# The dense tiles' hidden state kept in SBUF through the expert mixer, and the first block of U in other slots

## The chip, the cores and the metric

The kernel runs on one core of one Trainium2 chip, as one program, written in Python with a scheduler that orders the instructions of five engines and places their waits. The metric is the device time of the whole program in microseconds (us), the median of three runs. Engine names in the rows: PE is TensorE (PEld its weight loads), DVE is VectorE, ACT is ScalarE, POOL is GpSimd, SP is SyncE, which issues most DMAs; a q behind a name (SPq, ACTq) is the engine's issuing queue.

## The reference

One decoder layer over 512 tokens of width 1024, in float32:

```python
mod = silu(c) @ w_ada + b_ada                       # shift, scale, gate, twice
h   = rms_norm(x, norm1_g) * (1 + scale1) + shift1
proj = h @ w_in                                      # latent attention and forgetting attention
o   = concat(latent_attention(proj), forgetting_attention(proj))
x   = x + gate1 * (o @ w_o)
h2  = rms_norm(x, norm2_g) * (1 + scale2) + shift2
qp  = h2 @ w_pq                                      # 8 heads x 2 halves x 128
sc  = qp . sub_keys                                  # 128 keys per half
# top 16 of each half, top 16 of their sums -> 16 experts of 16384 per head and token
x   = x + gate2 * sum_e softmax(top)_e * gelu(peer_u[e] . h2) * peer_v[e]
```

## The kernel before, in words

The 512 tokens are four tiles of 128. Tile 0 is "sparse": its experts' rows of `peer_u` and `peer_v` are gathered from DRAM by GpSimd (L831) and used on VectorE (L849, L859). Tiles 1 to 3 are "dense": for all 384 tokens together TensorE computes every expert's `peer_u . h2` in 128 blocks of 128 experts (the U blocks, `dense_u`), and then the gated sum with `peer_v` in 128 blocks (`v_mm`, L981). A gate matrix G, built from the chosen experts, is written to DRAM and read back between the two.

Float32 products are three products of two rounded parts: ScalarE casts the high part (`hi`), VectorE subtracts it (`lo`), and TensorE runs hi·hi, hi·lo, lo·hi. For weights this is `halves` (L371 load, L373 `whi`, L374 `wlo`, products L385 to L387), for h2 L724 and L725, for a U or V block `split` (L871 `uhi`, L872 `ulo`), with the products of a U block in L935 to L937: 24 matmuls of 128x384.

The stages in order of time: a start (adaLN vectors, the first normalised tiles), projections and attention to 390 us, the queries (`queries`: four chunks of `w_pq`, 96 products of 128x384 each, then scores with the sub keys, L666), the U blocks (from 490 us to 1049 us), and the V blocks. The top 16 searches on VectorE (`top16`, L731 to L735) of the dense tiles run beside the queries and the first U blocks.

The order on each engine is made by the scheduler, which places an instruction when its operands and a slot for its result are there by its own clock; on the chip each engine then runs its list in that order and waits where a semaphore has not come. A DMA also waits until an older DMA that used the same of eight completion semaphores has landed. So a smaller pool or an absent DMA can move instructions far from the edited lines.

Memory around the change: `k4` is a pool of 28 slots of 4 KB per partition. It holds the split weights, and the mask, the rope table, the values `V` of the four tiles, and h2. `k4` is closed (`reopen`) when the U blocks begin, and the pool "dense" is opened in its place. h2 therefore goes to DRAM (`hd`) when it is made, 24 DMAs of 128 KB on ScalarE's queue (L727), and comes back into the new pool as `hhi` and `hlo`, 8 DMAs of 384 KB on GpSimd's queue (L884). The first U block is loaded in `reopen` too, after the pool has opened.

## Time and profile before

| | us |
|---|---|
| median of 3 runs (lowest, highest) | 1693.03 (1692.58, 1693.55) |
| the profiled execution | 1691.5 |
| its span in the trace | 1689.1 |
| TensorE busy | 1586.1 (94%) |
| VectorE busy | 1263.2 (75%) |
| ScalarE busy | 678.6 (40%) |
| GpSimd busy | 478.6 (28%) |

The time of an execution is about 2.4 us more than the span that the trace covers. Shares are averages over stages that have different limits: a stage is read from a window of its own, and from what ended the idle time in front of an engine's instructions.

### The profile page before, as it was taken

The page shows a single profiled execution, that of the slowest core. Times are in us where ns is not written, and L with a number is a line of the kernel's source. Part 1 is how long each engine was busy: PE and PEld are TensorE (multiplying, and loading weights), DVE is VectorE, ACT ScalarE, POOL GpSimd, SP SyncE. Part 2 cuts the span into 40 slices and gives each one's busy share as a digit, 9 for nine tenths or more (in the row PEclk, how much of TensorE's full clock was granted, in tenths as well). Part 3 has the DMA queues.
Part 4 walks back from the last instruction along what each step waited for, and adds up shares of the span by engine and source line. Part 5 has one row for each costly group of instructions (what it writes and reads, how often), then busy time and mean ns, then how long its engine had stood idle before and what let it go on. Part 6 is the DMA issues. An engine that isn't in the chain of part 4 may idle for free.

```text
span 1689.1 us, 25030 instructions
## 1 busy us (share of the span) xinstructions
PE 1586.1 (94%) x8993; PEld 1390.9 (82%) x8993; DVE 1263.2 (75%) x2626; ACT 678.6 (40%) x1072; POOL 478.6 (28%) x514
## 2 busy tenths in 40 slices
PE   5999999998978999999999999799999999999996
PEld 2976498987977999999999999787777777877885
DVE  2624364585899679899989899488888888887863
ACT  3522364354224434334656656333333333333331
POOL 1303510001013355564213232123333333233311
PEclk8999999999989999999999999999999999999998
DMA  7354513368154688888999999999999999999852
GB/s 295 122 212 159 194 39 132 121 215 272 36 188 139 229 287 264 262 281 270 346 335 337 328 325 349 387 354 368 353 370 357 366 365 358 366 375 364 289 180 100
DMA packets 189391, 451.34 MB, mean 267 GB/s; under 512 B 16594, under 2 KB 102610, under 8 KB 185172
## 3 DMA queue, kind: packets, MB, share of 16 engines
q1 hardware_dynamic: 91732, 277.17, 46.1%
q0 software_dynamic: 38656, 139.48, 23.5%
q10 hardware_dynamic: 58880, 33.11, 6.5%
q8 instruction: 70, 1.15, 0.3%
q14 instruction: 53, 0.43, 0.1%
HBM read 393.07 MB, written 56.63 MB: 266 GB/s over the span
## 4 chain that ended last, share of the span: by engine, by line
PE 75%; DVE 11%; DMA 7%; ACT 2%; issue 2%; POOL 0%; POOLq 0%; SPq 0%; DVEq 0%; ACTq 0%
PE acc L981 27%; PE bank L937 8%; PE bank L936 8%; PE bank L935 8%; PE bank L386 4%; PE bank L173 4%; PE bank L387 4%; PE bank L385 4%; DVE ulo L872 3%; PE bank L820 3%; DMA vt<-in_peer_v 2%; PE bank L136 2%; PE bank L564 2%; PE bank L579 2%; DMA ge<-ged 1%
## 5 line engine op out<-in xcount | busy, mean ns | idle before, releaser
L981 PE MATMUL acc<-vhi,whl 128*128 128x512 f32 x1536 | 422.6, 395 | 25.7 <-ACT vhi L871 17.0
L981 PEld LDWEIGHTS acc<-vhi,whl 128*128 128x128 f32 x1536 | 289.0, 189 | 94.1 <-ACT vhi L871 21.7
L937 PE MATMUL bank<-hhi,ulo 128*128 128x384 f32 x1024 | 348.0, 340 | 17.2 <-DVE ulo L872 17.2
L935 PE MATMUL bank<-hhi,uhi 128*128 128x384 f32 x1024 | 346.3, 339 | 12.3 <-ACT uhi L871 12.2
L936 PE MATMUL bank<-hlo,uhi 128*128 128x384 f32 x1024 | 348.3, 340 | 0.0
L831 POOL DMA_INDIRECT gat<-in_peer_v,ids x128 | 158.4, 1238 | 348.2 <-DVE y L859 324.2
L871 ACT CAST uhi<-ut 128x1024 fp32r<-128x1024 f32 x128 | 134.5, 1051 | 304.5 <-PE bank L936 262.4
L981 PE MATMUL acc<-vlo,whl 128*128 128x512 f32 x768 | 241.0, 395 | 0.1
L831 POOL DMA_INDIRECT gat<-in_peer_u,ids x128 | 142.6, 1114 | 336.0 <-DVE sact L849 305.1
L872 DVE TENSOR_TENSOR ulo<-ut,uhi 128x1024 fp32r<-128x1024 f32 x128 | 178.5, 1395 | 63.6 <-ACT uhi L871 62.8
L937 PEld LDWEIGHTS bank<-hhi,ulo 128*128 128x128 f32 x1024 | 194.3, 190 | 23.0 <-DVE ulo L872 22.6
L935 PEld LDWEIGHTS bank<-hhi,uhi 128*128 128x128 f32 x1024 | 194.3, 190 | 14.2 <-ACT uhi L871 13.8
L936 PEld LDWEIGHTS bank<-hlo,uhi 128*128 128x128 f32 x1024 | 194.5, 190 | 0.5
L872 DVE TENSOR_TENSOR vlo<-vt,vhi 128x1024 fp32r<-128x1024 f32 x128 | 156.4, 1222 | 43.6 <-ACT vhi L871 42.7
L871 ACT CAST vhi<-vt 128x1024 fp32r<-128x1024 f32 x128 | 133.7, 1049 | 110.6 <-PE acc L981 85.4
L981 PEld LDWEIGHTS acc<-vlo,whl 128*128 128x128 f32 x768 | 145.1, 189 | 33.1 <-DVE vlo L872 1.2
L859 DVE SCALAR_TENSOR_TENSOR y<-gat,swgt,y 128x1024 f32<-128x1024 f32 x127 | 167.8, 1322 | 1.8 <-DMA gat<-in_peer_v,ids 1.7
L971 ACT CAST whl<-ge 128x384 fp32r<-128x384 f32 x128 | 65.4, 512 | 257.4 <-PE acc L981 240.1
L849 DVE CUSTOM_DVE_ANT_0 scr<-gat,h2r 128x1024 bf16<-128x1024 f32 x128 | 166.2, 1298 | 0.1
L972 DVE TENSOR_TENSOR whl<-ge,whl 128x384 fp32r<-128x384 f32 x128 | 70.8, 555 | 55.6 <-ACT whl L971 52.4
L822 ACT ACTIVATE gst<-bank 128x512 f32<-128x512 f32 x96 | 96.8, 1117 | 9.3 <-PE bank L820 4.7
L968 DVE TENSOR_TENSOR ge<-ge,gt 128x384 f32<-128x384 f32 x128 | 69.8, 552 | 17.7 <-DMA ge<-ged 15.6
(252 smaller groups left out, 2217.2 us busy)
## 6 DMA issues: line engine op xcount, KB each, us to landing
ut<-in_peer_uT SPq DMA_DIRECT2D x128, 512.0 KB
vt<-in_peer_v SPq DMA_DIRECT2D x128, 512.0 KB
G<-gst ACTq DMA_DIRECT2D x24, 1024.0 KB
gt<-G SPq DMA_DIRECT2D x16, 1536.0 KB
ged<-ge SPq DMA_DIRECT2D x120, 192.0 KB
ge<-ged SPq DMA_DIRECT2D x120, 192.0 KB
w<-in_w_ada SPq DMA_DIRECT2D x16, 1024.0 KB
w<-in_w_pq SPq DMA_DIRECT2D x32, 512.0 KB
```

The costliest lines, as they stand in the source:

```text
L822: nc.scalar.activation(st[:, :, q + t4:q + t4 + 4].rearrange("p i t -> p t i"), pb.rearrange("p (t i) -> p t i", t=4), AF.Copy, scale=1.0 ...
L831: self.nc.gpsimd.indirect_dma_start(out=t, out_offset=None, in_=self.I[table], in_offset=bass.IndirectOffsetOnAxis(ap=ids[:, k:k + 1], axi ...
L849: v.tensor_tensor_reduce(out=scr, in0=u, in1=self.rows, op0=OP.mult, op1=OP.add, scale=1.0, scalar=0.0, accum_out=a[:, k:k + 1])
L859: v.scalar_tensor_tensor(out=self.y, in0=t, scalar=w[:, k:k + 1], in1=self.y, op0=OP.mult, op1=OP.add)
L871: nc.scalar.copy(hi, src)
L872: self.last_split = eng.tensor_tensor(out=lo, in0=src, in1=hi, op=OP.subtract)
L935: pe.matmul(A, uh[:, k, :], hh, start=(k == 0), stop=False)
L936: pe.matmul(A, uh[:, k, :], hl, start=False, stop=False)
L937: pe.matmul(A, ul[:, k, :], hh, start=False, stop=(k == KD - 1))
L968: nc.vector.tensor_tensor(out=wg, in0=wg, in1=self.gt[:, :, b % GI, :], op=OP.mult)
L972: nc.vector.tensor_tensor(out=wl, in0=w, in1=wh, op=OP.subtract)
L981: self.nc.tensor.matmul(self.acc[t][half], w[:, ts], v[:, half * 512:(half + 1) * 512], start=(b == n == 0), stop=(b == NK - 1 and n == 2))
```

## The change

- `k4` has 22 slots instead of 28. A new pool `kr` of 6 slots stands on the other ("right") side of SBUF and holds the mask, the rope table and the four `V`.
- When h2 of the first dense tile is made, that side is closed and a pool `hp` is opened in its place. It holds h2's eight tiles (`h2hi0` to `h2hi3`, `h2lo0` to `h2lo3`, 3 KB per partition each) to the end.
- The 24 DMAs to `hd` and the 8 back are gone, and `hd` with them; `dense_u` reads `h2hi` and `h2lo` directly.
- The first U block is loaded and split in `queries`, in the last chunk, into slots of the pool `ld` (4 slots, the raw `w_pq` weights' own), not in `reopen`.

```diff
-        self.k4p = self.top.enter_context(tc.tile_pool(name="k4", bufs=28))
+        self.k4p = self.top.enter_context(tc.tile_pool(name="k4", bufs=22))
+        self.side = ctx.enter_context(ExitStack())
+        with tc.using_default_side("right"):
+            self.krp = self.side.enter_context(tc.tile_pool(name="kr", bufs=6))
...
-        self.mask = self.k4([P, S], "mask")
+        self.mask = self.kr([P, S], "mask")
...
-        tab = self.k4([P, 4, NT, RD], "rope")
+        tab = self.kr([P, 4, NT, RD], "rope")
...
-        T["V"] = self.k4([P, 2, H, VD], "V")
+        T["V"] = self.kr([P, 2, H, VD], "V")
...
+            if j == 2 and c == 3:
+                self.us = {0: self.u_load(0)}
...
-            self.h2 = [[self.k4([P, 2, ND_T], x, F32R) for _ in range(KD // 2)] for x in ("h2hi", "h2lo")]
+            self.side.close()
+            with self.tc.using_default_side("right"):
+                hp = self.side.enter_context(self.tc.tile_pool(name="hp", bufs=1, reuse_waits="tile"))
+            self.h2 = [[hp.tile([P, 2, ND_T], F32R, name=f"{x}{q}") for q in range(KD // 2)] for x in ("h2hi", "h2lo")]
...
-            for z, h in enumerate((hi, lo)):
-                nc.scalar.dma_start(self.hd[z, :, 2 * q:2 * q + 2, ts], h.bitcast(F32))
...
-    def split(self, src, name, eng):
+    def split(self, src, name, eng, new=None):
...
-        hi, lo = (self.dn(src.shape, name + x, F32R) for x in ("hi", "lo"))
+        hi, lo = ((new or self.dn)(src.shape, name + x, F32R) for x in ("hi", "lo"))
...
-        hh = [[self.dn([P, 2, ND_T], f"{x}{q}", F32R, 1) for q in range(KD // 2)] for x in ("hhi", "hlo")]
-        self.us = {0: self.u_load(0)}
-        for q in range(KD // 2):
-            for z in range(2):
-                nc.gpsimd.dma_start(hh[z][q], self.hd[z, :, 2 * q:2 * q + 2, :])
-        self.h2 = hh
...
-        ut = self.dn([P, KD, P], "ut", F32, 3)
+        ut = self.ld([P, KD, P], "ut") if b == 0 else self.dn([P, KD, P], "ut", F32, 3)
         self.load(ut, self.I["peer_uT"][b])
-        return self.split(ut, "u", self.nc.vector)
+        return self.split(ut, "u", self.nc.vector, self.ld if b == 0 else self.dn)
```

Line numbers of the changed kernel are 3 to 9 higher.

The first place is ScalarE's list at the start, where `xn` is the square of a tile for its norm, `x` an eviction of a transposed tile, `hTh` a cast, and `whi` the cast that the first products of the projections wait for. Before:

```order
20 L304 COPY macc_219<-bank2_218 128x512
21 L243 DMA rg_315<-in_rope_g 128x64
22 L167 ACTIVATE x_139<-bank_251,b1_117,a1_116 128x128
23 L167 ACTIVATE x_149<-bank_275,b1_117,a1_116 128x128
24 L265 ACTIVATE ropework_319<-ropework_319 128x64 x2
25 L167 ACTIVATE x_139<-bank_251,b1_117,a1_116 128x128
26 L167 ACTIVATE x_149<-bank_275,b1_117,a1_116 128x128
27 L397 CAST hTh_260<-x_139 128x512
28 L397 CAST hTh_284<-x_149 128x512
29 L345 ACTIVATE xn_347,nss_348<-x_345 128x1024
30 L345 ACTIVATE xn_357,nss_358<-x_355 128x1024
31 L373 CAST whi_368<-w_366 128x768
```

and now:

```order
20 L310 COPY macc_221<-bank2_220 128x512
21 L249 DMA rg_317<-in_rope_g 128x64
22 L351 ACTIVATE xn_349,nss_350<-x_347 128x1024
23 L173 ACTIVATE x_141<-bank_253,b1_119,a1_118 128x128
24 L173 ACTIVATE x_151<-bank_277,b1_119,a1_118 128x128
25 L271 ACTIVATE ropework_321<-ropework_321 128x64 x2
26 L351 ACTIVATE xn_359,nss_360<-x_357 128x1024
27 L173 ACTIVATE x_141<-bank_253,b1_119,a1_118 128x128
28 L173 ACTIVATE x_151<-bank_277,b1_119,a1_118 128x128
29 L379 CAST whi_370<-w_368 128x768
30 L403 CAST hTh_262<-x_141 128x512
```

Both squares have moved ahead of the last two evictions, and `whi` ahead of the two casts `hTh`.

The second place is SP's list at the first U blocks (`ut`), with the semaphores each waits for (DMAHW is a completion semaphore of an older DMA). Before:

```order
120 L371 DMA w_4282<-in_w_pq 128x1024 [waits DMAHW3_49,DMAHW0_49,DVE_49]
121 L371 DMA w_4288<-in_w_pq 128x1024 [waits DMAHW4_49,DVE_49]
122 L281 DMA ut_4552<-in_peer_uT 128x1024 [waits DMAHW5_49,DVE_49,PE_49]
123 L281 DMA h2r_4566<-h2d_107 128x1024 [waits DMAHW6_49]
124 L281 DMA ut_4596<-in_peer_uT 128x1024 [waits DMAHW7_49]
125 L281 DMA ut_4655<-in_peer_uT 128x1024 [waits DVE_49,DMAHW0_49,PE_49,Pool_49]
```

and now:

```order
120 L377 DMA w_4264<-in_w_pq 128x1024 [waits DMAHW7_49,DVE_49]
121 L377 DMA w_4270<-in_w_pq 128x1024 [waits DMAHW0_49,DVE_49]
122 L287 DMA ut_4477<-in_peer_uT 128x1024 [waits DMAHW1_49,DVE_49]
123 L287 DMA h2r_4532<-h2d_109 128x1024 [waits PE_49]
124 L287 DMA ut_4562<-in_peer_uT 128x1024
125 L287 DMA ut_4621<-in_peer_uT 128x1024 [waits DVE_49,PE_49]
```

The first `ut` no longer waits for TensorE, and the second follows `h2r`, which waits for a product of the third query chunk; no DMA of `hd` stands in what they wait for.

The third place is VectorE's list where the V blocks begin: `ge` times the gate `gt`, the low parts `whl` and `vlo`, and the gathered rows of the sparse tile (`scr`, `y`). Before:

```order
1462 L968 TENSOR_TENSOR ge<-ge,gt 128x384
1463 L972 TENSOR_TENSOR whl<-ge,whl 128x384
1464 L968 TENSOR_TENSOR ge<-ge,gt 128x384
1465 L872 TENSOR_TENSOR vlo<-vt,vhi 128x1024
1466 L849 ISA scr,sact<-gat,h2r 128x1024
1467 L849 ISA sact 128x1
1468 L968 TENSOR_TENSOR ge<-ge,gt 128x384 x2
1469 L972 TENSOR_TENSOR whl<-ge,whl 128x384
```

and now:

```order
1459 L970 TENSOR_TENSOR ge<-ge,gt 128x384
1460 L881 TENSOR_TENSOR vlo<-vt,vhi 128x1024
1461 L858 ISA scr,sact<-gat,h2r 128x1024
1462 L858 ISA sact 128x1
1463 L974 TENSOR_TENSOR whl<-ge,whl 128x384
1464 L970 TENSOR_TENSOR ge<-ge,gt 128x384 x5
1465 L881 TENSOR_TENSOR vlo<-vt,vhi 128x1024
1466 L868 SCALAR_TENSOR_TENSOR y<-gat,swgt,y 128x1024
```

From here on the same instructions stand in another mixture, as `vhi` and `whl` do on ScalarE; between the first sixteen U blocks and this place the list is the same but for a few neighbours.

## Rows read from the trace of the kernel before

**Rows 1.** The page: busy time by engine, and one costly group.

```profile
PE 1586.1 (94%) x8993; PEld 1390.9 (82%) x8993; DVE 1263.2 (75%) x2626; ACT 678.6 (40%) x1072; POOL 478.6 (28%) x514
...
L981 PE MATMUL acc<-vhi,whl 128*128 128x512 f32 x1536 | 422.6, 395 | 25.7 <-ACT vhi L871 17.0
```

**Rows 2.** Windows: length, busy time of PE, PEld, DVE, ACT, POOL; clock, DMA, GB/s.

```profile
40.00:395.00 355.00, 348.38 (x2212) 285.26 (x2213) 183.14 (x605) 149.03 (x348) 67.29 (x118) 0.99 0.43 151
430.86:483.47 52.61, 52.61 (x322) 52.61 (x322) 51.06 (x331) 11.96 (x23) 4.13 (x16) 1.00 0.01 2
483.47:574.13 90.66, 72.98 (x399) 70.16 (x398) 78.02 (x337) 32.36 (x43) 28.79 (x40) 0.91 0.68 221
574.13:611.57 37.44, 37.44 (x218) 37.44 (x217) 23.58 (x51) 15.88 (x22) 10.08 (x11) 1.00 0.79 265
488.00:492.00 4.00, 0.00 (x0) 0.00 (x0) 3.93 (x25) 0.58 (x2) 0.00 (x0) 0.77 1.08 388
496.00:500.00 4.00, 2.83 (x9) 2.83 (x10) 3.03 (x17) 1.04 (x1) 0.00 (x0) 0.50 1.09 400
```

**Rows 3.** Timeline of TensorE at the start: start, length, line, [idle before].

```profile
41.90 1.01 PE L385 MATMUL bank<-whi,hTh 128*128 128x384 f32 x2 [9.85 <-ACT whi L373]
...
45.17 0.69 PE L386 MATMUL bank<-wlo,hTh 128*128 128x384 f32 x1 [0.37 <-DVE wlo L374]
```

**Rows 4.** Timeline of ScalarE at the start.

```profile
30.36 0.58 ACT L304 COPY macc<-bank 128x512 f32<-128x512 f32 x1 [1.01 <-PE bank L303]
...
38.94 1.05 ACT L345 ACTIVATE xn<-x 128x1024 f32<-128x1024 f32 x1
...
41.04 0.81 ACT L373 CAST whi<-w 128x768 fp32r<-128x768 f32 x1
```

**Rows 5.** Timeline of VectorE at the start.

```profile
32.68 0.15 DVE L321 SCALAR_TENSOR_TENSOR a<-a,cols 128x4 f32<-128x4 f32 x1
...
36.38 0.22 DVE L276 SCALAR_TENSOR_TENSOR rope<-ropework,rg 128x64 f32<-128x64 f32 x1 [2.26 <-DMA rg<-in_rope_g]
...
37.47 0.72 DVE L165 TENSOR_SCALAR x<-bank,a,b 128x128 f32<-128x128 f32 x2
42.02 0.75 DVE L347 TENSOR_SCALAR xn<-x,nrs 128x1024 f32<-128x1024 f32 x1 [3.84 <-POOL nrs L128]
...
44.17 0.95 DVE L374 TENSOR_TENSOR wlo<-w,whi 128x768 fp32r<-128x768 f32 x1
```

**Rows 6.** Timeline of TensorE at the entry to the queries.

```profile
398.60 1.09 PE L136 MATMUL bank<-ident,xn 128*128 128x128 f32 x8 [2.07 <-DVE xn L347]
...
407.75 1.65 PE L385 MATMUL bank<-h2hi,whi 128*128 128x384 f32 x4 [5.69 <-ACT h2hi L724]
```

**Rows 7.** Timeline of ScalarE at the same place.

```profile
395.68 1.06 ACT L345 ACTIVATE xn<-x 128x1024 f32<-128x1024 f32 x1 [1.21 <-DVE h2lo L725]
```

**Rows 8.** Waits of the SP queue, 385 to 430 us: total, times, longest.

```profile
SPq L371 <- DMA xd<-x: 12.5, 1, 12.5
...
SPq L371 <- DMA hd<-h2hi: 6.3, 1, 6.3
```

**Rows 9.** Timeline of TensorE at the hand-over to the U blocks.

```profile
492.63 0.69 PE L935 MATMUL bank<-hhi,uhi 128*128 128x384 f32 x1 [5.18 <-ACT uhi L871]
497.17 0.69 PE L935 MATMUL bank<-hhi,uhi 128*128 128x384 f32 x1 [3.86 <-ACT uhi L871]
...
514.32 0.69 PE L937 MATMUL bank<-hhi,ulo 128*128 128x384 f32 x1 [3.83 <-DVE ulo L872]
```

**Rows 10.** Chain of waits, 482 to 500 us: start, length, what.

```profile
484.44 11.62 DMA ut<-in_peer_uT
```

**Rows 11.** Timeline of VectorE, the low halves of three U blocks.

```profile
574.13 1.23 DVE L872 TENSOR_TENSOR ulo<-ut,uhi 128x1024 fp32r<-128x1024 f32 x1
...
578.29 1.23 DVE L872 TENSOR_TENSOR ulo<-ut,uhi 128x1024 fp32r<-128x1024 f32 x1
...
611.57 2.25 DVE L872 TENSOR_TENSOR ulo<-ut,uhi 128x1024 fp32r<-128x1024 f32 x1 [1.31 <-ACT uhi L871]
```

More of the change, by code (lines that the diff above doesn't have):

```diff
@@ L103, in k4, with kr @@
         return self.k4p.tile(list(shape), dt, name=name, tag="k4")
+    def kr(self, shape, name, dt=F32):
+        return self.krp.tile(list(shape), dt, name=name, tag="kr")
     def ld(self, shape, name, dt=F32):
@@ L875, in reopen @@
     def reopen(self):
-        nc = self.nc
         self.top.close()
         self.dp = self.top.enter_context(self.tc.tile_pool(name="dense", bufs=1, reuse_waits="tile"))
-        hh = [[self.dn([P, 2, ND_T], f"{x}{q}", F32R, 1) for q in range(KD // 2)] for x in ("hhi", "hlo")]
-        self.us = {0: self.u_load(0)}
-        for q in range(KD // 2):
-            for z in range(2):
-                nc.gpsimd.dma_start(hh[z][q], self.hd[z, :, 2 * q:2 * q + 2, :])
-        self.h2 = hh
         self.rows = self.dn([P, D], "h2r", F32, 1)
@@ L929, in dense_u @@
         pe = nc.tensor
-        uh, ul = self.us.pop(b) if b in self.us else self.u_load(b)
+        uh, ul = self.us.pop(b, None) or self.u_load(b)
         pa = self.bank() if b < AHEAD else self.bank2()
@@ L1003, in build @@
         T = [{} for _ in range(NT)]
-        self.hd = self.dr.tile([2, P, KD, ND_T], F32, name="hd")
         self.h2d = self.dr.tile([P, D], F32, name="h2d")
```

## The prediction

> **What bounds the kernel now.** I read the page first: TensorE is busy for 94% of the span, VectorE for 75% [rows 1]. So the change can only be worth what TensorE stands still or runs slow in the stages that it touches, and what the stages behind them don't take back. Windows by stage come next [rows 2]. From 40 to 395 us TensorE is idle for 355.00 - 348.38 = 6.6 us in all: a microsecond won at the start is carried to the queries. In the queries (430.86 to 483.47) TensorE never stops and VectorE is busy for 51.06 of 52.61 us. From 483.47 to 574.13, the hand-over to the U blocks, TensorE is idle for 90.66 - 72.98 = 17.7 us and VectorE for 90.66 - 78.02 = 12.6. From 574.13 on TensorE never stops again in that stage, and a U block takes 578.29 - 574.13 = 4.16 us [rows 11]. So there are three places with something to win: the start, the entry to the queries, the hand-over. TensorE's timelines show what its gaps wait for: 9.85 us for `whi` at 41.90 [rows 3], 2.07 for `xn` and 5.69 for `h2hi` at the entry [rows 6], and 5.18, 3.86 and 3.83 for `uhi` and `ulo` at the hand-over [rows 9].
>
> **The start.** The edit of the pools moves the two squares on ScalarE ahead, and `whi` ahead of the casts `hTh`. Before, the squares (from 38.94, each 1.05) and the casts stood between VectorE's late `x` and `whi` at 41.04 [rows 4]. That `x` was late because the rope operations wait in front of it for the DMA `rg`, landed at 36.38 [rows 5]; this DMA is still issued behind ScalarE's copy that ends at 30.36 + 0.58 = 30.94, so I leave its landing. Now the first square runs in the idle time until the vector `a` is there (32.68 + 0.15 = 32.83); behind it come two pairs of evictions (0.72 a pair, VectorE's row), the second square 1.05 and two sines (0.4, an estimate from the 0.2 of such small operations in the same rows): 32.83 + 1.44 + 1.05 + 0.4 = 35.7, and `whi` (0.81) ends at 36.5 instead of 41.85. The products proper start with `wlo`, though: rope from 36.38, `x` to 37.47 + 0.72 = 38.2, one `xn` 0.75, `wlo` 0.95: 39.9 instead of 44.17 + 0.95 = 45.12. That is 5.2 us at best. Against it, the norm's factor comes from GpSimd (`xn` began 0.9 us behind the end of both squares, at 42.02), and the smaller pool lets the last loads of the start go out only when TensorE has freed their slots. I take 3, nearer to the best end since the rows give every step, with bounds of -2 (a load that comes as late as two casts or squares of 1.05 take) and 5.2.
>
> **The entry to the queries.** Eight issues of `hd` and four casts stood on ScalarE in front of the squares of the last two tiles, which began at 395.68 [rows 7]; TensorE got their `xn` 2.07 us late. In the new order all three squares stand ahead, and TensorE has other work until then, so this gap goes. The loads of `w_pq` lose the waits for landings: 12.5 us behind `xd`, 6.3 behind `hd` [rows 8], most of it hidden by TensorE's queue of work. The gap of 5.69 keeps its evictions and casts, but two of the four `whi` and the issues are out of its way. I take 3 in all; the bounds are 0 (the same gap, later) and 2.07 + 5.69 = 7.8.
>
> **The hand-over.** Removed are the eight loads of `hhi` and `hlo` (3 MB), and the wait of the first `ut` for the last query products. In the chain of waits the second `ut` takes 11.62 us to land [rows 10], with the DMA engines full (1.08 and 1.09 of their time at 388 and 400 GB/s) and TensorE's clock granted at 0.50, its lower level of 1.2 GHz, behind its standstill [rows 2]. Now the first two are there before the query products end, and U block 0 follows the scores at once. The Trainium skill, page "DMA: Bandwidth & Descriptors", section "Anatomy of one DMA", puts a DMA at about 2.0 us and its bytes at 436 GB/s, an estimate of 3.2 us for these 512 KB; the trace's 11.62 is far from it, as a queue behind other transfers is. By that rule as by the row the new second load is in time, being issued a chunk earlier.
>
> What ends last then is VectorE. In front of the `ulo` of block 16 (574.13) its list holds the same work in both kernels, 78.02 us from 483.47 on [rows 2], of which one `ulo`, 1.23, has moved into the idle time before. If it never waited, block 16 would come at 483.47 + 78.02 - 1.23 = 560.3, which is 13.9 us earlier. TensorE by itself would allow its 17.7 us of idle time and some 3 more for the half clock (an estimate from 2.83 busy us at 0.50 in one window of four [rows 2]), so 21. But VectorE takes its list in order, and where it comes to a `ulo` whose `uhi` waits for an older block on TensorE it stands: of the 12.6 us of idle time I leave about 4, giving 10. I choose near the VectorE bound because in the queries, with the same mixture of searches, it was idle for 1.6 of 52.61 us [rows 2]. Bounds: 1 (all of the 12.6 idle us stay, only the moved `ulo` is won) and 21.
>
> The rest costs nothing that I can find: U blocks from 16 on stand in the same order at TensorE's pace, and h2's tiles are read from another address only.
>
> **Sum.** 3 + 3 + 10 = 16 us, off the profiled execution's 1691.5: 1675.5. That execution was 1.5 us below the median of the runs (1693.03), so 1677 for a median. The bounds of the terms add to -1 and 34.
>
> **The rivals.** (1) VectorE keeps most of its waits at the hand-over, since blocks and searches are interleaved for the scheduler's clock and not the chip's: the term is 2, the sum 8, the time 1685. For it: the 12.6 us of idle time now; against it: 10 of them would have to come back while TensorE has two blocks in hand.
> (2) TensorE's full pace is reached, because searches slip behind block 16 in fact: start 5, entry 3, hand-over 21, time 1664. Against it: the list in front of block 16 holds all of them.
> (3) VectorE's subtractions get slower: the `ulo` at 611.57, among gathers, took 2.25 where the two before took 1.23 [rows 11]. If the six blocks from 11 to 16 meet that, 6 x 1.02 = 6 of the 10 go, the sum is 10 and the time 1683. The Trainium skill, page "GPSIMD Engine Reference", section "8. Key points", says that GpSimd shares its SBUF interfaces with VectorE and contends with VectorE's operations on two SBUF inputs, which `ulo` is; no row here shows that it is the cause.
> (4) Slower: from the first V block on, `ge`·`gt`, `whl`, `vlo` and `vhi` stand in another mixture on VectorE and ScalarE. TensorE's idle time in front of the V products is 25.7 us now, 17.0 of it for `vhi` [rows 1]. If the new mixture makes `vhi` late as often again, 25.7 us are lost and the time is 1677 + 25.7 = 1703. It decides from the point where that idle time grows by more than 16. Against it: the stage has the same operations, and a mixture can gain as well.
> (5) No change: what is won is taken back by a wait that doesn't move with the rest, such as the G matrix's round trip before the first V block: 1692. Against it: TensorE doesn't stop once from 574.13 to 611.57 [rows 2], so what is won stands at the end of that stretch in full.
>
> **How the numbers follow.** Forecast 0.57, rivals (1) 0.17, (2) 0.05, (3) 0.06, (4) 0.08, (5) 0.07. A change within 0.2% (3.4 us) is about what a measurement of this kernel can't tell from none. Faster is the forecast with (1), (2) and (3): 0.85; the same is (5), 0.07; slower is (4), 0.08. For eight times in ten the range takes the forecast's own 1669 to 1683 and goes up to (1) with some of its spread, 1688, and down to 1665 for (2).
>
> **What would show it.** In the profile after: the gap at 41.90 at some 36 to 37 and shorter by 3 to 5 us; the one of 2.07 gone and the first `h2hi` product at about 401 to 403 (both earlier terms together); no gap over 2 us between the scores and the second U block, no clock of 0.50 there; `ulo` of block 16 at about 558, with VectorE idle for some 4 us in front of it where it was 12.6; TensorE's idle time at L981 near 25.7. I am wrong if block 16 comes less than 8 us earlier than the entry did, if the idle time at L981 has grown by 10 or more, or if the first projections start no earlier.

## The result: 1683.9 us, and the profile after

The kernel after took 1683.91 us, median of five runs (1681.4 to 1686.75), against 1693.03 before (1692.58 to 1693.71): ratio 0.9948, 95% interval 0.9933 to 0.9962. Run again on another chip it took 1683.72 against 1692.24, ratio 0.9950 (0.9936 to 0.9963). The gain is 9.1 us in the medians, against a forecast of 16 (1677). The profiled execution took 1681.4 us, 10.1 less than that of before.

First the page of after (busy time, and the V products' group). TensorE works as long as before; its idle time ahead of the V products is 29.1 us [rows 1: 25.7], so rival (4) did not come.

```profile
PE 1585.8 (94%) x8993; PEld 1390.0 (83%) x8993; DVE 1265.0 (75%) x2626; ACT 678.2 (40%) x1072; POOL 483.3 (29%) x506
...
L983 PE MATMUL acc<-vhi,whl 128*128 128x512 f32 x1536 | 422.3, 394 | 29.1 <-ACT vhi L880 17.0
```

The same engine work finishes earlier, so the gain is a sum of shifts: the start of one and the same instruction in after, less its start in before. That is the lead (minus is earlier). The 41st query product is the first of those that stand behind all gaps of the entry. TensorE timelines and VectorE's for `ulo`, `vlo`, give for after and for every experiment below:

| lead, us | last projection product | 41st query product | last query product | `ulo` of block 20 | first `vlo` | last `vlo` |
|---|---|---|---|---|---|---|
| (before, start) | 388.12 | 416.86 | 484.44 | 590.77 | 1057.07 | 1667.07 |
| after | -3.0 | +0.3 | +0.3 | -9.6 | -10.0 | -9.0 |
| after, again (e10) | -1.8 | +1.5 | +1.5 | -8.3 | -8.4 | -7.3 |
| e1 late w_pq | -5.8 | -5.9 | -5.9 | -13.1 | -13.1 | -12.2 |
| e5 w_pq in g8 | -6.4 | -6.0 | -6.0 | -18.8 | -18.7 | -20.7 |
| e9 e5 + GpSimd | -6.0 | -5.6 | -5.6 | -17.5 | -18.9 | -22.5 |
| e2 less sorting | -0.8 | +2.8 | +2.8 | -10.3 | -10.1 | -8.3 |
| e3 late block 0 | -2.4 | +1.0 | +0.9 | -8.2 | -8.3 | -5.5 |
| e8 writes back | -1.8 | -1.8 | -1.8 | -10.7 | -11.0 | -7.6 |
| e4 pools only | -3.1 | +0.6 | +0.6 | -1.8 | -1.9 | -2.3 |
| e11 e4 + g8 | -6.4 | -5.3 | -5.2 | -5.8 | -5.5 | -3.7 |
| e6 spread | -2.4 | +1.2 | +1.1 | -8.1 | +2.8 | +1.1 |
| e7 e1 + spread | -6.8 | -7.3 | -7.3 | -16.2 | -5.4 | -18.3 |

At 288 us, behind the start, all twelve are 4.5 to 6.8 us ahead (after 6.7). What differs is how much of that reaches the queries, and what the hand-over adds. Each row is one profiled execution, and these lie up to 4.4 us off the median of their kernel (e2 +4.4, e6 +4.0, e8 and e11 +3.4, e5 -3.4, after -2.5), so the rows compare stages, and times are compared by the ratios further down.

**The start.** TensorE's timeline: the first products of `whi` at 37.36 with a gap of 4.42 [rows 3: 41.90, 9.85], the first of `wlo` at 39.73 [45.17], 5.4 us earlier. ScalarE's square at 31.73 runs where it was idle, and `whi` is at 36.48 [rows 4: 41.04]. VectorE still waits for `rg`, at 36.20 [rows 5: 36.38].

```profile
37.36 1.01 PE L391 MATMUL bank<-whi,hTh 128*128 128x384 f32 x2 [4.42 <-ACT whi L379]
...
39.73 0.67 PE L392 MATMUL bank<-wlo,hTh 128*128 128x384 f32 x1
```

```profile
31.73 1.06 ACT L351 ACTIVATE xn<-x 128x1024 f32<-128x1024 f32 x1
...
36.48 0.83 ACT L379 CAST whi<-w 128x768 fp32r<-128x768 f32 x1
```

```profile
36.20 0.23 DVE L282 SCALAR_TENSOR_TENSOR rope<-ropework,rg 128x64 f32<-128x64 f32 x1 [0.91 <-DMA rg<-in_rope_g]
```

**The output projection.** Here the lead falls from 6.65 to 2.98 us between the products at 364 and 385 us. On TensorE's timeline four gaps wait for low halves of the weights, and then one for `xn`. Before has no gap for `wlo` there. VectorE's timeline, second, shows that it stood idle itself, until a product on TensorE (the bank of L392) was done.

```profile
366.40 0.50 PE L392 MATMUL bank<-wlo,oTh 128*128 128x512 f32 x1 [0.39 <-DVE wlo L380]
...
371.24 0.50 PE L392 MATMUL bank<-wlo,oTh 128*128 128x512 f32 x1 [0.47 <-DVE wlo L380]
...
376.53 0.50 PE L392 MATMUL bank<-wlo,oTh 128*128 128x512 f32 x1 [0.92 <-DVE wlo L380]
...
381.83 0.50 PE L392 MATMUL bank<-wlo,oTh 128*128 128x512 f32 x1 [0.92 <-DVE wlo L380]
388.64 1.96 PE L142 MATMUL bank<-ident,xn 128*128 128x128 f32 x8 [3.11 <-DVE xn L353]
390.40 8.12 PE L179 MATMUL bank<-x,w 128*128 128x128 f32 x64
398.36 1.91 PE L142 MATMUL bank<-ident,xn 128*128 128x128 f32 x16
```

```profile
369.96 1.23 DVE L380 TENSOR_TENSOR wlo<-w,whi 128x1024 fp32r<-128x1024 f32 x1 [2.29 <-PE bank L392]
375.25 1.22 DVE L380 TENSOR_TENSOR wlo<-w,whi 128x1024 fp32r<-128x1024 f32 x1 [4.07 <-PE bank L392]
380.55 1.22 DVE L380 TENSOR_TENSOR wlo<-w,whi 128x1024 fp32r<-128x1024 f32 x1 [4.08 <-PE bank L392]
```

That is a circle: TensorE waits for a low half, and that waits for TensorE to let go of a slot. The slots are short although `kr` took its own tiles along: these are read for the last time at 218.8 us (rope), 351.1 (mask) and 354.3 (`V`) in before, where `k4` then has their six slots for the weights; in after they stay in `kr`, done with at 347.6, until `hp` takes their place.

**The entry.** Another 3.3 us go. The gap of 2.07 in front of the `xn` of the last two tiles [rows 6] is gone: their 16 transposes at 398.36 follow the 64 products of L179 without one. But a gap of 3.11, the last of those above, stands in front of the first tile's `xn`, where before had none:

```profile
388.35 1.03 PE L136 MATMUL bank<-ident,xn 128*128 128x128 f32 x8
389.22 7.31 PE L173 MATMUL bank<-x,w 128*128 128x128 f32 x64
```

(before). The low halves come late to all three tiles, so the first tile is done no earlier than in before (ScalarE begins its square at 385.17, before at 384.76), while TensorE's last projection product comes 3.0 us earlier. Behind that gap the clock is granted at a mean of 0.58 from 388 to 392 us, where before has 1.00 (first after, then before), and the 8 transposes and 64 products take 0.93 and 0.81 us longer:

```profile
388.00:392.00 4.00, 3.36 (x16) 3.36 (x17) 2.62 (x5) 2.79 (x8) 3.75 (x6) 0.58 0.37 150
388.00:392.00 4.00, 4.00 (x36) 3.87 (x35) 3.09 (x7) 2.41 (x6) 0.00 (x0) 1.00 0.63 230
```

The gap before the first `h2hi` product is hardly shorter, 5.46 [rows 6: 5.69], and a second one of 1.07 follows.

```profile
406.62 1.65 PE L391 MATMUL bank<-h2hi,whi 128*128 128x384 f32 x4 [5.46 <-ACT h2hi L735]
409.33 0.69 PE L392 MATMUL bank<-h2lo,whi 128*128 128x384 f32 x1 [1.07 <-DVE h2lo L736]
```

On ScalarE's timeline two copies of w_pq stand ahead of the cast that the first product waits for, one of them behind a wait for its load; before had four, from 399.73 to 404.86. The `h2lo` of the second gap waited for no other engine: a `wlo` of w_pq and searches stand ahead of it in VectorE's list.

```profile
401.43 1.04 ACT L379 CAST whi<-w 128x1024 fp32r<-128x1024 f32 x1 [1.54 <-DMA w<-in_w_pq]
404.84 1.07 ACT L379 CAST whi<-w 128x1024 fp32r<-128x1024 f32 x1
406.14 0.73 ACT L735 CAST h2hi<-x 128x256 fp32r<-128x256 f32 x2
```

```profile
406.38 1.21 DVE L380 TENSOR_TENSOR wlo<-w,whi 128x1024 fp32r<-128x1024 f32 x1
...
408.88 0.41 DVE L736 TENSOR_TENSOR h2lo<-x,h2hi 128x256 fp32r<-128x256 f32 x1
```

**The hand-over.** U block 0 follows the scores at once, and 9.8 us are won. One gap of 4.06 is left, for the `ulo` of block 1; behind it the clock is again granted at 0.50, 1.2 GHz, for a stretch. `ulo` of block 16 comes at 566.59 [rows 11: 574.13].

```profile
496.70 0.69 PE L939 MATMUL bank<-h2hi,ulo 128*128 128x384 f32 x1 [4.06 <-DVE ulo L881]
```

```profile
566.59 1.21 DVE L881 TENSOR_TENSOR ulo<-ut,uhi 128x1024 fp32r<-128x1024 f32 x1
```

Windows of after for the stretches of [rows 2] (length, busy time of PE, PEld, DVE, ACT, POOL, clock, DMA share, GB/s). From the start of the last query product to block 16 it is 81.89 us, where it was 574.13 - 484.44 = 89.7 (the row of [rows 2] begins 1 us ahead of that product): 7.8 less. VectorE is idle for 81.89 - 78.64 = 3.3 of them (12.6 before), TensorE for 8.9 (17.7).

```profile
431.00:484.70 53.70, 53.70 (x329) 53.70 (x328) 51.19 (x331) 12.12 (x24) 2.92 (x13) 1.00 0.08 24
484.70:566.59 81.89, 73.02 (x405) 70.10 (x405) 78.64 (x336) 32.98 (x43) 25.50 (x34) 0.96 0.58 184
566.59:603.00 36.41, 36.41 (x212) 36.34 (x211) 24.64 (x54) 14.36 (x20) 11.09 (x11) 1.00 0.85 285
496.00:500.00 4.00, 3.30 (x10) 3.30 (x11) 4.00 (x23) 0.00 (x0) 0.00 (x0) 0.50 0.46 135
```

### The profile page after: what moved, and what is told of

It reads as the page before. It is cut to its first block, busy times and chain, and to the rows that moved or that the text cites. A ratio compares the mean times of both kernels' runs of the same rounds, so it can differ in the third digit from the quotient of the medians.

```text
span 1679.6 us, 24979 instructions
## 1 busy us (share of the span) xinstructions
PE 1585.8 (94%) x8993; PEld 1390.0 (83%) x8993; DVE 1265.0 (75%) x2626; ACT 678.2 (40%) x1072; POOL 483.3 (29%) x506
## 4 chain that ended last, share of the span: by engine, by line
PE 74%; DVE 17%; DMA 4%; issue 3%; ACT 2%; POOL 0%; POOLq 0%; DVEq 0%; ACTq 0%; SPq 0%
PE acc L983 29%; PE bank L939 8%; PE bank L938 7%; PE bank L937 7%; PE bank L179 4%; DVE ulo L881 3%; PE bank L392 3%; PE bank L391 3%; PE bank L829 3%; PE bank L393 3%; PE bank L142 3%; DMA ge<-ged 2%; PE bank L570 2%; PE bank L585 2%; DVE scr L858 1%
## 5 line engine op out<-in xcount | busy, mean ns | idle before, releaser
L983 PE MATMUL acc<-vhi,whl 128*128 128x512 f32 x1536 | 422.3, 394 | 29.1 <-ACT vhi L880 17.0
L983 PEld LDWEIGHTS acc<-vhi,whl 128*128 128x128 f32 x1536 | 288.7, 189 | 97.5 <-ACT vhi L880 21.7
L939 PE MATMUL bank<-h2hi,ulo 128*128 128x384 f32 x1024 | 349.1, 341 | 19.6 <-DVE ulo L881 19.6
L938 PE MATMUL bank<-h2lo,uhi 128*128 128x384 f32 x1024 | 349.1, 341 | 0.0
L937 PE MATMUL bank<-h2hi,uhi 128*128 128x384 f32 x1024 | 346.6, 338 | 0.0
L840 POOL DMA_INDIRECT gat<-in_peer_v,ids x128 | 162.9, 1273 | 333.1 <-DVE y L868 311.8
L983 PE MATMUL acc<-vlo,whl 128*128 128x512 f32 x768 | 240.7, 394 | 0.7 <-DVE vlo L881 0.7
L939 PEld LDWEIGHTS bank<-h2hi,ulo 128*128 128x128 f32 x1024 | 193.8, 189 | 26.9 <-DVE ulo L881 26.5
L938 PEld LDWEIGHTS bank<-h2lo,uhi 128*128 128x128 f32 x1024 | 193.8, 189 | 0.5
L937 PEld LDWEIGHTS bank<-h2hi,uhi 128*128 128x128 f32 x1024 | 193.7, 189 | 0.5
L983 PEld LDWEIGHTS acc<-vlo,whl 128*128 128x128 f32 x768 | 145.1, 189 | 33.5 <-DVE vlo L881 1.5
L970 DVE TENSOR_TENSOR ge<-ge,gt 128x384 f32<-128x384 f32 x128 | 69.8, 553 | 18.3 <-DMA ge<-ged 16.3
```

Of the source, the lines that this page charges most:

```text
L840: self.nc.gpsimd.indirect_dma_start(out=t, out_offset=None, in_=self.I[table], in_offset=bass.IndirectOffsetOnAxis(ap=ids[:, k:k + 1], axi ...
L937: pe.matmul(A, uh[:, k, :], hh, start=(k == 0), stop=False)
L938: pe.matmul(A, uh[:, k, :], hl, start=False, stop=False)
L939: pe.matmul(A, ul[:, k, :], hh, start=False, stop=(k == KD - 1))
L970: nc.vector.tensor_tensor(out=wg, in0=wg, in1=self.gt[:, :, b % GI, :], op=OP.mult)
L983: self.nc.tensor.matmul(self.acc[t][half], w[:, ts], v[:, half * 512:(half + 1) * 512], start=(b == n == 0), stop=(b == NK - 1 and n == 2))
```

## The experiments

Each was timed beside runs of the kernel before on its chip. e1 to e4 share one chip, e5 to e8 another, e9 to e11 a third; so their ratios are compared, not their times.

| run | us, median | ratio to before, 95% |
|---|---|---|
| after | 1683.91 | 0.9948 (0.9933 to 0.9962) |
| e1 | 1676.89 | 0.9897 (0.9882 to 0.9912) |
| e2 | 1677.47 | 0.9907 (0.9891 to 0.9923) |
| e3 | 1683.42 | 0.9933 (0.9919 to 0.9947) |
| e4 | 1689.93 | 0.9981 (0.9972 to 0.9990) |
| e5 | 1673.10 | 0.9888 (0.9872 to 0.9904) |
| e6 | 1687.48 | 0.9973 (0.9964 to 0.9981) |
| e7 | 1674.12 | 0.9895 (0.9880 to 0.9910) |
| e8 | 1679.57 | 0.9919 (0.9904 to 0.9933) |
| e9 | 1669.67 | 0.9871 (0.9856 to 0.9887) |
| e10 (after) | 1683.72 | 0.9950 (0.9936 to 0.9963) |
| e11 | 1684.61 | 0.9955 (0.9941 to 0.9968) |

### e1: w_pq's first chunk behind the projections

```diff
-run(pipe(o[:3] + [prep(self.w_pq, 0)] + o[3:5] + n[:1] + o[5:] + [prep(self.w_pq1, 3)] + n[1:] + [q1(3)], 2))
+run(pipe(o[:5] + n[:1] + o[5:] + [prep(self.w_pq, 0), prep(self.w_pq1, 3)] + n[1:] + [q1(3)], 2))
```

> The kernel after, with the load and split of the first chunk of w_pq moved from behind the third to behind the last output projection, and nothing else. In the kernel after, TensorE runs 6.7 us ahead of the kernel before until 365 us and 2.0 us behind it at 398 us. Theory 1 (slots): the 22 slots of k4 are then held by oT (6), the first half of w_o (8) and the eight low parts of w_pq, so that the low parts of the second half of w_o wait for products to free theirs. Without w_pq ahead of them they wait for less: the gaps on TensorE with the releaser DVE wlo between 365 and 385 us (0.39, 0.47, 0.92, 0.92 us) go, at least 4 of the 8.7 us come back, the first product of h2hi starts before 403 us and the time is 1676 to 1680 us. Theory 2 (order and loads: the scheduler's order of the projections or the landing of w_o's second half makes the loss): the projections end no earlier; the chunk of w_pq comes later instead, the first h2hi product stays at 406 us or slips to 408 to 412, and the time is 1684 to 1689 us.

Measured: 1676.89 us, as theory 1 had it, and the four gaps are gone. Of TensorE's waits from 360 to 400 us (total, times, longest) one line stays, for loads of the one sparse tile's weights:

```profile
PE bank L179 <- DMA w<-in_w_pq: 4.7, 3, 2.0
```

The lead is 5.8 us at the last projection and 5.9 in the queries: neither the projections nor the entry take any of it. But the edit moves both slots and order, so e5.

### e5: the same slots freed, the order kept

```diff
+if name == "w_pq0" and k < 4:
+    g = self.g8p.tile([P, 2, 2, n], F32R, name="whl", tag="g")
+    hi, lo = g[:, 0], g[:, 1]
+else:
     hi, lo = new([P, 2, n], "whi", F32R), self.k4([P, 2, n], "wlo", F32R)
```

> The kernel after, its order of tasks kept, with the high and low parts of the first two row pairs of w_pq's first chunk in the two 8 KB slots of the pool g8, which nothing holds between 150 and 420 us, so that four more slots of k4 are there for the second half of w_o. Theory 1 (the projections' loss is a shortage of slots, whatever the order): about as in the run with the late w_pq: the second half of w_o is split earlier, the shift against the kernel before at the last output projection is -4 to -6 us instead of -2 to 0, and the time is 1677 to 1681 us. Theory 2 (what helped there was the place of w_pq's split in the order on ScalarE and VectorE, ahead of or behind the second half of w_o, not the slots): the shift at the last output projection stays between -2.5 and +1 us and the time at 1682 to 1686 us.

Measured: 1673.10 us, below what either theory gave, and the lead at the last projection 6.4 us, where theory 1 asked for 4 to 6. The gaps for `wlo` are gone; TensorE's waits from 360 to 400 us are one line, a wait for the entry that now begins earlier:

```profile
PE bank L395 <- ACT h2hi L739: 6.8, 1, 6.8
```

So it is the slots: four more at that place, and the code's order unchanged, give the whole loss back (the engines' lists move with the slots, as the scheduler makes them). The same waits tell it in all runs: in after, e2, e3, e4, e6, e8 and e10 the line for `wlo` between 365 and 400 us is the same,

```profile
PE bank L392 <- DVE wlo L380: 2.7, 4, 0.9
```

and it isn't there in before, e1, e5, e7, e9 and e11. The same seven runs, and no other, have the entry's gap of 3.1 for `xn`. The line accounts for 2.7 of the 3.7 us, and the rest stands at the same four places, where the lead falls by 0.5, 0.8, 1.2 and 1.2. Products overlap, so a gap counted from the end of one is shorter than what it costs: the one at 376.53 starts 1.31 us behind the one before, where products of this stretch start 0.23 apart, which is 1.08 lost in a gap of 0.92. The Trainium skill, page "Perfetto Trace Analysis", section "Identifying Performance Opportunities", says that a gap repeating at the same size on the engine that should be full can mean too little SBUF for the next tile. The gaps (0.92, 0.92; on VectorE 4.07, 4.08) agree.

e5 also won more at the hand-over, 12.8 us where after has 9.8 and e1 only 7.2; VectorE was idle for 78.06 - 76.54 = 1.5 us in it. In e1 the same stretch (478.54 to 562.94) holds 80.3 us of VectorE's work instead of 76.5, and 4.1 idle; why more was left for it there was not tried. e5's row:

```profile
478.44:556.50 78.06, 70.67 (x399) 68.63 (x399) 76.54 (x334) 29.65 (x41) 25.49 (x34) 0.98 0.64 209
```

### e4 and e11: the pools alone, without and with the slots

```diff
-self.k4p = self.top.enter_context(tc.tile_pool(name="k4", bufs=28))
+self.k4p = self.top.enter_context(tc.tile_pool(name="k4", bufs=22))
+self.side = ctx.enter_context(ExitStack())
+with tc.using_default_side("right"):
+    self.krp = self.side.enter_context(tc.tile_pool(name="kr", bufs=6))
```

(with `mask`, `rope` and `V` from `kr`, on the kernel before; e11 has e5's edit besides.)

> The kernel before with the split of the pool alone: k4 of 22 slots and kr of 6 on the right side (for the mask, the rope table and the three values); h2 stays in k4 and goes through memory, and the first block of U is loaded as before. Theory 1 (the start's gain and the loss in the output projection both come from the slots and the order that they give): TensorE's first matrix work starts 4 to 5 us earlier, is 5 to 7 us ahead at 145 us, and has lost at least 6 of it by 398 us; the hand-over with its gap of 17.15 us stays, h2 takes 8 of the 22 slots, and the time is 1692 to 1697 us. Theory 2 (the start's gain and the later loss come from the other edits, by the scheduler's new order): TensorE's first work stays within 1 us of 41.90 and the time is 1691 to 1694 us with no loss between 365 and 398 us.

> The kernel of e4 (before, with k4 of 22 and kr of 6 slots; h2 in k4 and through memory) with the four parts of w_pq's first chunk in g8. Theory 1 (the start's lead comes from the split pool, and the slots decide how much of it reaches the queries): at the last output projection 5 us or more of the lead are left (e4: 3.1), the queries end 3 to 6 us earlier than in the kernel before (e4: 0.56 later), the hand-over keeps its long gap since h2 still goes through memory, and the time is 1684 to 1688 us. Theory 2 (with h2 in the same 22 slots there is shortage either way): as e4, 1689 to 1691 us.

Measured: e4 1689.93 us, faster than either theory said, since 2.3 us came at the hand-over, which I had left as it was; why was not tried. Its first products stand at 36.22, 5.7 us earlier than before, so the pools alone give the start's lead; at the queries it has gone (+0.6). e11 keeps 5.2 to 5.3 us of it in the queries and takes 1684.61, in the range of theory 1. Its hand-over still waits for h2 (TensorE's waits, 478 to 575 us):

```profile
PE bank L946 <- DMA hhi<-hd: 8.3, 1, 8.3
PE bank L948 <- DVE ulo L882: 5.8, 6, 1.6
PE bank L947 <- DMA hlo<-hd: 3.1, 3, 1.6
```

Start and hand-over are thus two separate gains: e4 and e11 win 2.3 and 0.6 at the hand-over, the kernels with h2 in SBUF and all the work 7.2 to 12.8.

### e3 and e8: which part of the hand-over's edit

e3 puts U block 0 back behind the opening of the pool `dense`; e8 puts the 24 writes of `hd` back, unread; with the 8 reads gone it moves 3 MB less than before, not the 6 that its expectation names.

```diff
-if j == 2 and c == 3:
-    self.us = {0: self.u_load(0)}
```

```diff
+for z, h in enumerate((hi, lo)):
+    nc.scalar.dma_start(self.hd[z, :, 2 * q:2 * q + 2, ts], h.bitcast(F32))
```

> The kernel after, with the first block of U loaded and split where the kernel before has it (after the pool dense is opened, from that pool) instead of among the queries; h2 stays in SBUF. Theory 1 (most of the 10 us of the hand-over come from VectorE no longer waiting, and the round trip of h2 was what it waited for): the early block is worth 1 to 4 us at most, because only the first ulo of 1.6 us and the load of its 512 KB come late; a gap of 3 to 8 us opens on TensorE behind the last scores, VectorE fills it with sorting, block 16's ulo comes 0 to 3 us later, and the time is 1684 to 1687 us. Theory 2 (the early first block is what saves the 10 us): block 16 comes 6 to 10 us later (573 to 577) and the time is 1690 to 1694 us.

> The kernel after with the 24 writes of h2 to memory put back on ScalarE's queue, and nobody reads them (6 MB of transfers less than the kernel before: only the reads are gone). Theory 1 (the writes' part of the gain lies at the entry alone, their issue on ScalarE beside the normalisation, and the hand-over gains by the missing reads and waits): first h2hi product 1 to 2.5 us later than in the kernel after (406.62), block 16 as much later, time 1685 to 1687 us. Theory 2 (the writes cost nothing, being on queues that wait for nothing): within 1 us of the kernel after, 1683 to 1685 us. Theory 3 (the writes hold up ScalarE's queue and the U loads): more than 4 us later, over 1688 us.

Measured: e3 1683.42 us, hand-over 9.1 instead of 9.8, so theory 1 held in the main (its times began at 1684, and its gap of 3 to 8 us behind the scores did not come, the longest is 2.2): the early block is worth 0.7 us in the profile, nothing in the median. e8 took 1679.57, which no theory foresaw; its ratio, 0.9919, is below that of after, 0.9948, by intervals that just touch. Its hand-over wins 8.9, and its entry costs nothing (1.8 ahead at both ends) where after loses 3.3. It has the gap of 3.11 too and the slow clock behind it, so it wins back by its order what these take: five evictions and a cast stand ahead of the first copy of w_pq on ScalarE where after has two evictions, and one copy, not two, ahead of the cast for the first product. The gap before that product is 3.50 instead of 5.46, and there is none for `h2lo`:

```profile
403.47 1.04 ACT L379 CAST whi<-w 128x1024 fp32r<-128x1024 f32 x1 [0.92 <-DMA w<-in_w_pq]
...
405.42 0.70 ACT L735 CAST h2hi<-x 128x256 fp32r<-128x256 f32 x2
```

```profile
405.87 1.37 PE L391 MATMUL bank<-h2hi,whi 128*128 128x384 f32 x4 [3.50 <-ACT h2hi L735]
```

So most of the gain at the hand-over comes from what reads h2 back, the loads and their waits: with the writes still there it is 8.9 of 9.8. Taking the writes away won nothing by itself at the entry; it gave the scheduler another order. That order alone, without the writes, was not tried.

### e2, e6, e7 and e9: is VectorE the bound?

e2 leaves out half of the maxima of the dense tiles' last chunk:

```diff
+if i != SPARSE and c == 3:
+    self.nc.vector.max(out=T["tv"][:, h, z, :8], in_=T["sc", c][:, j, :])
+    self.nc.vector.max_index(out=T["ti"][:, h, z, :8], in_max=T["tv"][:, h, z, :8], in_values=T["sc", c][:, j, :])
+    continue
```

> The kernel after, in which the last chunk of scores of the three dense tiles gets only its first eight maxima (the other eight are copied from them, so the choice of experts is another one): some 12 us less work of VectorE (24 pieces of 0.29 + 0.28 + 0.28 + 0.17 us, less 6 copies) among the first U blocks, nothing else. Theory 1 (the hand-over is bound by VectorE): the gaps of 0.45 to 0.87 us on TensorE with releaser DVE ulo between 496 and 560 us shrink, block 16's ulo starts 5 to 8 us earlier than in the kernel after (566.59), where TensorE (8.2 us idle of 77 from 483 to 560) becomes the bound, and the time is 1676 to 1679 us. Theory 2 (it is bound by the order of the queues or the loads of U, not by VectorE's work): block 16 comes within 2 us of 566.6 and the time stays at 1683 to 1685 us.

Measured: 1677.47 us; the hand-over wins 13.1 us instead of 9.8, so 3.3 of the 12 us of work that went; its start gave 2.2 us less than after's, which is why block 20 stands at only -10.3. TensorE's waits for `ulo` from 483 to 567 us fall from 8.9 to 6.4. Of these, 4.0 are the one gap of block 1, while VectorE is now idle for 76.6 - 64.6 = 12.0 us up to block 16 (487.20 to 563.80). So VectorE bounds the hand-over, but only for about 3 us of the 12; behind that first gap 2.4 us are left on TensorE for less sorting to win.

e6 spaces the same work out; e7 does so on e1:

```diff
-work = seq(pick(0), *(top(i, c) for c in (2, 3) for i in DENSE), *(pick(i) for i in DENSE),
+work = seq(pick(0), spread(seq(*(top(i, c) for c in (2, 3) for i in DENSE)), 2), *(pick(i) for i in DENSE),
```

> The kernel after with the six sorting steps of the dense tiles' last two chunks of scores given out at every second U block instead of at every one (108 steps over 112 blocks instead of 102); nothing is left out. Theory 1 (VectorE bounds the first U blocks): VectorE's load per block falls, TensorE's gaps of 0.45 to 0.87 us with releaser DVE ulo between 500 and 560 us shrink by half or more, block 16's ulo starts 2 to 5 us earlier relative to the first projections, and the time is 1679 to 1682 us. Theory 2 (the scheduler fills VectorE with whatever is ready, so the spacing in the code changes little; or the choices for the gates come too late instead): within 1.5 us of the kernel after, 1682.5 to 1685.5 us.

> Both edits on the kernel after: w_pq's first chunk behind the last output projection, and the sorting steps at every second U block. If the two losses are separate, their gains add: 1676.9 less 2 to 4 us, 1673 to 1675 us. If VectorE's sorting only moves to another place where TensorE waits for it, it stays at 1676 to 1678 us.

Measured: e6 1687.48 us, worse than after and outside both ranges. e7 1674.12: that lies in the range for gains that add, but on a chip where before ran 1691.97, and its ratio, 0.9895, is level with e1's 0.9897. Theory 1 of e6 fell: its hand-over wins 9.3, and VectorE is still busy for 30.00 of 30 us from 530 to 560. What theory 2 named last, choices that come too late, is in the trace: the lead of 12.7 us in the last U blocks turned into a lag of 2.8 at the first `vlo` (on TensorE the first V product is still 1.1 us ahead). There VectorE waits from 1030 to 1120 us for the first gate matrix (before and after wait there for `ge`, up to 9.9 and 11.9 us at once):

```profile
DVE ge L970 <- DMA gt<-G: 16.3, 1, 16.3
```

```profile
DVE ge L970 <- DMA ge<-ged: 12.3, 2, 11.9
```

(e6's first, then after's.) In e7 the lead on TensorE falls in the same way, from 20.9 us in the last U blocks to 11.8 at the first V product, and then grows to 18.3 at the last; no run here says why.

e9 moves six subtractions of the queries to GpSimd, on e5:

```diff
+eng = self.nc.gpsimd if name in ("w_pq1", "w_pq2", "w_pq3") and k > 2 else self.nc.vector
+eng.tensor_tensor(out=lo, in0=w, in1=hi, op=OP.subtract)
```

> The kernel of e5 (four parts of w_pq's first chunk in g8), with the low parts of the third and fourth row pair of w_pq's second to fourth chunk made by GpSimd instead of VectorE: six pieces of 1.22 us less on VectorE, on an engine that is idle but for some 3 us between 400 and 483 us. Theory 1 (from 365 to 560 us VectorE is the bound, its idle time there sets when the U blocks run: in eight kernels alike in work, block 20's ulo comes 1.1 to 1.2 us earlier for each us more that VectorE is busy in that stretch): 4 to 7 us earlier at block 20 than e5, time 1667 to 1670 us. Theory 2 (GpSimd takes 2 us or more for such a piece and slows VectorE beside it, or TensorE waits for the late parts among the queries): a gap on TensorE with releaser POOL wlo between 430 and 480 us, block 20 no earlier than in e5, time 1673 us or more.

Measured: 1669.67 us, by its ratio not told apart from e5. The time lies in the range of theory 1 by luck: block 20 came no earlier (-17.5 against -18.8), so theory 1 is wrong as I put it. The six pieces ran between 402 and 438 us (its lines: count, ns min, median, max):

```profile
L385 POOL TENSOR_TENSOR wlo<-w,whi x6: 2383/2396/3615, 402.3 to 438.4; 128x1024 fp32r<-128x1024 f32 x6
L385 DVE TENSOR_TENSOR wlo<-w,whi x5: 1208/1225/1668, 399.4 to 421.1; 128x1024 fp32r<-128x1024 f32 x5
```

There VectorE isn't full: from 400 to 440 us it waits 7.8 us for ScalarE's `whi` and 3.2 for `uhi`. From 440 to 475 us, with the scores of the first chunks to sort, it is busy for 34.2 of 35 us. Work taken off before that is not work off the bound. On the price, the Trainium skill's page "GPSIMD Engine Reference", section "4.1 Engine selection", gives about twice VectorE's time for an operation with two inputs; the medians, 2396 and 1225 ns, agree.

### e10: after once more

> The kernel after once more, unchanged, with another profile, beside the versions made from it. If its profile of before is typical: TensorE's first work at 37 to 38 us, 1 to 3 us of the start's lead left at the last output projection, block 20's ulo at 581 +-1.5 us, and 1682 to 1685 us. If the stages vary by the run (as the spread of its times, 1681.4 to 1686.8 us, may mean), block 20 differs by more than 2 us from 581.2.

Measured: 1683.72 us. The start gave 5.5 instead of 6.7, the projections took the same 3.7, the entry the same 3.3, the hand-over gave the same 9.8. So the two profiles differ at the start, and from there to block 20 the stages repeat within 0.1 us; behind it this one lost 1.0 where the first lost 0.6.

## Why the prediction was right in sign and 7 us too high

- **The start**, forecast 3: it gave 4.5 at the first `whi` products, 5.4 at the first `wlo` product, where my best end was 5.2, and 6.7 at 288 us (5.5 in the second profile), above the term's bound. I had marked it down for GpSimd's factor and for loads that need slots; neither showed. Where the last microsecond before 288 us comes from was not asked.
- **The step that failed**: "a microsecond won at the start is carried to the queries". I read it from TensorE's small idle time from 40 to 395 us [rows 2]. That row tells that nothing was late there with 28 slots. The change takes six of them; I asked what that does to the loads of the start, not to the second half of w_o, which is split behind w_pq's first chunk. It took 3.7 us (e5 gives them back, e1 also).
- **The entry**, forecast 3: it lost 3.3. The gap of 2.07 went, as I had said, and two of four copies left the place in front of `h2hi`. But "TensorE has other work until then" was wrong for the first tile: the three tiles end together, and a gap of 3.11 with 1.7 us of slow clock behind it came instead. From there to `h2hi` 0.9 were won, at the `h2lo` and behind it 1.4 lost: 3.11 + 1.7 - 2.07 - 0.9 + 1.4 is the 3.3. With enough slots the entry costs nothing (e1, e5: within 0.4 us of before), and gains nothing either: the 3 us were not there. First product at 406.62 instead of 401 to 403.
- **The hand-over**, forecast 10: 9.8 in both profiles. Its reason held too: VectorE idle for 3.3 us in front of block 16 where I left 4. Two signs were wrong: there is a gap of over 2 us (4.06, the `ulo` of block 1 stood behind sorting) and a stretch at 0.50. The `ulo` of block 16 came at 566.6, not 558, as the entry was later. From the last query product it came 7.8 earlier, by block 20 9.8; by my own sign, "less than 8 us earlier than the entry did", the forecast is missed by 0.2. TensorE's products of block 16 do come 9.6 us earlier than before's, as those of block 20, so this `ulo` was late for no one. The section "Anatomy of one DMA" on the page "DMA: Bandwidth & Descriptors" of the Trainium skill, which I cited for the load, gives its fit for DMAs that GpSimd issues. `ut` is issued by SyncE; no term went by it.
- **Later**, forecast 0: 0.6 lost between block 20 and the last V block; the idle time at L983 grew by 3.4 [rows 1].

So +6.7, -3.7, -3.3, +9.8 and -0.6: 8.9 us, which is the lead at the last `vlo`. That the time fell within the range owes something to luck: the start's surplus of 3.7 paid for the projections' loss of 3.7, and of the 7 us that are missing the entry has 6.3. Rivals (1) and (3) gave a time near the measured one by other ways, and neither way is in the profile: VectorE's waits at the hand-over went, and its `ulo` was not slower (1.48 us in the mean, 1.61 before; the last section has what makes single ones slow). The cause, in a word: the forecast counted what the change gives and priced the six slots that it takes at one place only.

## What to carry to other kernels

When a pool is cut, list for every later stage what holds its slots at the peak, above all prefetched weights that stand ahead of weights needed sooner: an engine that waits in gaps of one repeating size, for a producer that itself waits for that engine, is the sign. A small idle time says that a stage has no wait with the buffers it has, not that it passes a lead on with fewer. And taking work off a busy engine pays only in the stretch in which that engine is the bound: see where its list is full, and what it waits for where it is not. These three are drawn from this one kernel.

The best version, e5 (0.9888, or e9, 0.9871), takes the change and lends the two 8 KB slots of a pool that is idle at that point to four parts of the prefetched weights.

## What was not expected of the hardware

GpSimd's subtraction of 128x1024 took 2.40 us in the median where VectorE's takes 1.23 (e9); of the five on VectorE in that stretch four took 1.21 to 1.23 us and one 1.67. VectorE's `ulo` ran up to 2.59 us before 560 us in after (555.56) and up to 3.27 later (704.65); the mean from 483 to 560 us was 1.48 us, 1.61 before.

Rival (3) put such slow ones to gathers, and the traces say otherwise. Of after's 292 subtractions of this form (`ulo`, `vlo` and `wlo`) the 167 with no GpSimd instruction beside them took 1.23 us at most, and so did the 84 with nothing but gathers beside them. All 14 above 1.4 us overlap a product `prod` (L781) that GpSimd runs itself, and in all thirteen traces no slow one is without an elementwise operation of GpSimd's on two tensors. Beside such an operation 25 more stayed under 1.4 us, and the order of the starts tells most of them apart: in 12 of the 14 `prod` had begun first, as at 511.61 below, and all 14 ended 1.1 us behind `prod`'s end. Where the subtraction began first, as at 528.76, it took its 1.2 us and `prod` 2.5 instead of 1.6. (Two of the 14 began before `prod`, and one `prod` that began first, by 0.06 us, was itself the slow one; GpSimd's times in a trace are rough.)

```profile
511.61 1.63 POOL L781 TENSOR_TENSOR prod<-hit,cid 128x800 f32<-128x800 f16 x1 [28.64 <-DVE hit L778]
511.81 2.51 DVE L881 TENSOR_TENSOR ulo<-ut,uhi 128x1024 fp32r<-128x1024 f32 x1
...
528.76 1.21 DVE L881 TENSOR_TENSOR ulo<-ut,uhi 128x1024 fp32r<-128x1024 f32 x1
528.98 2.48 POOL L781 TENSOR_TENSOR prod<-hit,cid 128x800 f32<-128x800 f16 x1 [5.60 <-DVE hit L778]
```
